# A two-layer hybrid decoder trunk: layer 1's first stage in a written order, the gate's mix made in the keys, the values' buffers opened at the layer's beginning

## The chip, the cores and the metric

The kernel runs on one core of a Trainium2 chip. Its engines each work through a queue of their own, in order: TensorE (PE) multiplies matrices, with the loads of its stationary operand shown apart as PEld; VectorE (DVE), ScalarE (ACT) and GpSimd (POOL) work on elements; SyncE (SP) issues nearly all the DMA transfers. The metric is the device time of one execution in microseconds (us). Three runs took 2486.44 to 2488.04 us, median 2487.72.

## What is computed

A sequence of 512 tokens of width 2048 (batch 1) passes through two layers. Layer 0 is an attention with forget gates. Layer 1 is RWKV-7 time mixing, cut here to what matters:

```
xx = shift(h) - h                       # the token before, minus this one
xr, xw, xk, xv, xa, xg = (h + xx * mu[i] for i in 0..5)
r, k, v, z = xr @ w_in[0], xk @ w_in[1], xv @ w_in[2], xg @ w_in[3]
decay = exp(-exp(-softplus(-(w0 + tanh(xw @ w1) @ w2)) - 0.5))
v = v + (v_first - v) * sigmoid(v0 + (xv @ v1) @ v2)     # v_first: layer 0's values
a = sigmoid(a0 + (xa @ a1) @ a2)
kk = normalised(k * k_k);  k = k * (1 + (a - 1) * k_a)
S = S * w_t + (S a_t) b_t + v_t k_t;  y_t = S r_t        # 512 steps, 32 heads of 64
y = groupnorm(y) + (r * k * r_k) summed * v
out = (y * silu(z)) @ w_out;  x = x + gate * out
```

`h` is the normalised `x`, scaled and shifted per channel by a modulation made from `c` (`w_mod`). All is float32.

## The kernel before, in words

Activations lie with channels on the 128 partitions: 16 tiles `k` of 128 channels by 512 tokens. Every large matmul is made of three in a faster format: operand and weight are each split into a high part (a copy by ACT, `hi` or `whi`) and a low part (the difference, by DVE, `lo` or `wlo`), and PE multiplies hi by hi, hi by wlo and lo by whi (`mm3`). Weights come by SP into `raw` buffers ahead of that. One output tile of a projection (128 channels) is 16 `mm3`, 48 matmuls, accumulated in one PSUM bank.

**Layer 1's first stage** (pool `st1`) goes over the 16 tiles `k`. Each step makes the normalised `xn` (DVE) and `hp` (ACT: `xn` plus shift, with a leading zero column, so that `hp[:, 0:T]` is the tokens one earlier), stores `hp` to the DRAM tensor `h1d`, makes the difference `d` (DVE) and from it three mixes: the key's, `d * mu + hp` on DVE, split into `A[k]`; and the receptance's (n = 0) and the gate's (n = 5), a product on ACT and an addition on POOL, stored to `mxd[1]` and `mxd[2]`. Then 18 matmuls use `A[k]` for the first six tiles of the key projection, in six PSUM banks at once (named `pj`, `x`, `S`). Its weights are the tensor `wst1`, 128 x 768 a step.

**Order.** For each engine the class `InOrder` can fix the order of the instructions as the program writes them (`e.on`). It is off in this stage, so that the scheduler orders it, and on before and after it.

**The rest of layer 1** is one stream of projection tiles for PE, written by `backbone`: 10 key tiles, 16 of the receptance (`wr`), 16 of the values (`wv1`), 16 of the gate (`wz1`), 16 of the output (`wo1`). Beside it run tasks (Python generators) that the planner `Flow` starts when its clock `fl.t` has reached their time. The clock counts PE's matmuls, and steps on by 0.2 where PE has none. A task's `yield 5` leaves 5 of these units before its next instructions. `backbone` gives a bank to tile `i` only when tile `i-2` is in `freed`. The task `side` goes through the phases, each with a pool of buffers of its own: the low-rank projections (`lora_k`; it also makes the values' mix), their second halves (`lora_up`), the keys (`keys`, started `KEY` = 9.8 units apart), and the recurrence (`stage`, `stage_half`, `chain`, pool `rk`), which opens when all `qd` are there.

- `keys(j)` loads the inner sums `ip`, the key `kt` and `aa`, makes normalised and decayed keys, stores them, and multiplies them into `gab`. After four keys, `invert` inverts small triangular blocks by elementwise work on POOL (on DVE for the last group, `DG`), tile `lane`, stored to `qld`. `inverse` then loads these into `qt` (SP) and finishes them with matmuls. It is started `INV` units after the group's last key, or `DINV + 8` for the last group.
- `values(j)` blends the values with layer 0's, in tiles `sv`, `vf` and `vt`, and stores `vvd` and `vtd`. Its buffers come from the pool `rk`, so it first waits for `vqs`, and it counts as ended for `freed` when its last instruction is written.
- `stage` loads what a head pair's recurrence needs (some 20 DMAs), among it `vtd`, for which it waits (`vd`). `chain(j)` is the recurrence of tile `j`: 8 chunks of 64 tokens, three hops each, a hop not before the next multiple of `HOP` = 2.15. A chain may start 12 hops after the one before. Its first operation reading PSUM is the copy `xs`, its end the copy `ys`, a norm, and the store to `ypd`.
- `gated(j)` multiplies `silu(z)` with `yp`; the output tiles need all 16 of these.
- `mixing(i, ...)` loads a stored mix back (`mxd`, tile `hp`, five buffers counted by the token `m`) and splits it for the projection; `premixed` says which are stored.

Of the kernel before, what the change touches and what calls it, by code (L numbers as in the profile page):

```python
# [17 lines left out]
P = 128  # L18
# [111 lines left out]
def body(ctx, tc, a, out, dbg=None, stop=0):  # L130
# [52 lines left out]
    mraw = cp.tile([P, 6, 2 * KT], F, name="mraw")  # L183
# [11 lines left out]
    pool.tensor_scalar(oka, vecs[:, V_KA, :], -1.0, 1.0, op0=OP.mult, op1=OP.add)  # L195
    lnb = cp.tile([P, 1], F, name="lnb")
# [67 lines left out]
    def mod_unit(mp, cb, l, part, t):  # L264
        for h in range(2):
            s = slice(h * D // 2, (h + 1) * D // 2)
            w = mp.tile([P, D // 2], F, tag="wm", name="wm", bufs=3)
            sp.dma_start(w, a["wmodT"][l, part * KT + t][:, s])
            yield 4.5
            dve.tensor_tensor_reduce(out=w, in0=w, in1=cb[:, s], scale=1.0, scalar=0.0,  # L270
                                     op0=OP.mult, op1=OP.add,
                                     accum_out=mraw[:, 3 * l + part, 2 * t + h:2 * t + h + 1])
            mdone.add((l, part, t, h))
        m0, m1 = (mraw[:, 3 * l + part, 2 * t + h:2 * t + h + 1] for h in range(2))
# [112 lines left out]
    with ExitStack() as s0:  # L387
# [209 lines left out]
        def until(i):  # L597
            while i is not None and i not in ends:
                yield 0.2
# [316 lines left out]
        for e in (pe, dve, act):  # L916
            e.on = False
# [13 lines left out]
        with tc.tile_pool(name="st1", bufs=2, reuse_waits="tile") as q:  # L931
            for k in range(KT):
                xp = q.tile([P, T + 1], F, tag="xn", name="xn")
                xn = xp[:, 1:]
                pool.tensor_scalar(xp[:, 0:1], shift[:, 1, k:k + 1], -1.0, 1.0, op0=OP.mult,
                                   op1=OP.mult)
                dve.scalar_tensor_tensor(out=xn, in0=x1[k], scalar=scale[:, 1, k:k + 1],
                                         in1=rstd1, op0=OP.mult, op1=OP.mult)
                hp = q.tile([P, T + 1], F, tag="hp", name="hp")
                pool.memset(hp[:, 0:1], 0.0)  # L940
                act.activation(hp[:, 1:], xn, AF.Identity, bias=shift[:, 1, k:k + 1])
                sp.dma_start(h1d[k], hp)
                w = wload(a["wst1"][k:k + 1].rearrange("k p n -> p k n"), 1, NS1, "s", q)
                A.append(new_act(k))
                d = q.tile([P, T], F, tag="d", name="d")
                dve.tensor_tensor(out=d, in0=xp[:, 0:T], in1=xn, op=OP.subtract)
                m = q.tile([P, T], F, tag="m", name="m")
                dve.scalar_tensor_tensor(out=m, in0=d, scalar=vecs[:, V_MU + 2, k:k + 1],
                                         in1=hp[:, 1:], op0=OP.mult, op1=OP.add)
# [19 lines left out]
    mq = ctx.enter_context(tc.tile_pool(name="mq", bufs=2, reuse_waits="tile"))  # L969
    pools = ExitStack()  # L970
# [75 lines left out]
    premixed = {(i, k) for i in (1, 2) for k in range(KT)}  # L1046
# [115 lines left out]
    def values(j, o, e):  # L1162
        while not vqs:
            yield 0.2
        vq = vqs[0]
# [3 lines left out]
        vv = load(vq, vfT[j], "vf", bufs=2)  # L1169
        yield from until(e)  # L1170
# [5 lines left out]
        dve.tensor_tensor(out=vv, in0=vv, in1=o, op=OP.add)  # L1176
        yield 3
# [13 lines left out]


# [3 lines left out]
    def keys(q, j):  # L1196
# [3 lines left out]
        yield 5  # L1200
# [429 lines left out]
    INV, KEY = 50, 9.8  # L1630

    def side(q):
# [45 lines left out]
        vqs.append(rk)  # L1678
# [25 lines left out]
    vqs = []  # L1704
# [40 lines left out]
```

## Time and profile before

| | before |
|---|---|
| median of 3 runs | 2487.72 us |
| profiled execution | 2484.87 us, its span 2483.2 us |
| mean granted TensorE clock | 0.979 |
| PE busy | 2342.1 us, 94%, 13626 matmuls |
| PEld | 1812.4 us, 73% |
| DVE | 1658.1 us, 67%, 3114 instructions |
| ACT | 1242.7 us, 50%, 2281 instructions |
| POOL | 756.2 us, 30%, 1199 instructions |
| DMA | 476.06 MB, mean 192 GB/s |

How to read its rows: a row of a timeline is start, duration, engine, line, operation, output<-inputs, shape, count; in brackets stands how long the engine was idle before it and what released it. A row of a group gives count, then busy time and mean ns of one, then the idle time before them. A row of a window gives the busy time of each engine with its instruction count. All instructions are issued through one helper, so that every row has its line, L88. PE's ends are modelled, and neighbouring matmuls overlap: their distance from start to start is what counts. In layer 1 the first stage lies near 1104 to 1207 us of the span, the keys near 1370 to 1612, the recurrence from 1700 on.

### The profile page before, as it was taken

Reading aid. Unit: us, or ns where it says so; the run is one execution under the profiler, and the core shown is the slowest. Engines: PE = TensorE matmul, PEld = TensorE weight load, DVE = VectorE, ACT = ScalarE, POOL = GpSimd, SP = SyncE. Lnnn points to the kernel's source line nnn. Section 1 sums busy time; section 2 is a strip of 40 time slices with the busy share of each in tenths; the row PEclk is TensorE's granted clock in tenths of the full one; section 3 lists DMA queues with packets and bytes.
Section 4 is the critical chain, followed back from the end, with each engine's and each line's share of the span. In section 5 each row is a group of like instructions: output and inputs, shape, how many; then the busy total and the mean of one; then the engine's idle time right before and its main releaser. Section 6 shows DMA issues by size and latency. Waiting matters only on the chain. (4 is left out here: it accounts for less than half of the span.)

```text
span 2483.2 us, 39895 instructions
## 1 busy us (share of the span) xinstructions
PE 2342.1 (94%) x13626; PEld 1812.4 (73%) x13626; DVE 1658.1 (67%) x3114; ACT 1242.7 (50%) x2281; POOL 756.2 (30%) x1199
## 2 busy tenths in 40 slices
PE   7998999999999999987999998887999999999999
PEld 4786677787777888865766776765777767777787
DVE  7878787888887553349796666572577876776332
ACT  3426655555556552226447676642344545555321
POOL 0003424433332200117340248720434444441000
PEclk8999999999999999999999999998999999999999
DMA  8856566666664275436657886776656656554453
GB/s 315 314 210 208 179 198 215 208 211 202 211 202 153 94 234 173 146 117 215 193 168 254 264 253 213 215 209 188 199 156 174 194 155 180 158 146 154 142 148 98
DMA packets 339260, 476.06 MB, mean 192 GB/s; under 512 B 146288, under 2 KB 156656, under 8 KB 335216
## 3 DMA queue, kind: packets, MB, share of 16 engines
q1 hardware_dynamic: 337392, 470.88, 60.5%
q0 software_dynamic: 1664, 2.63, 0.3%
q8 instruction: 108, 1.77, 0.3%
q14 instruction: 96, 0.79, 0.1%
HBM read 377.42 MB, written 95.95 MB: 191 GB/s over the span
## 5 line engine op out<-in xcount | busy, mean ns | idle before, releaser
L88 PE MATMUL pj<-hi,whi 128*128 128x512 f32 x2416 | 990.4, 410 | 16.8 <-ACT hi L88 10.3
L88 PE MATMUL pj<-hi,wlo 128*128 128x512 f32 x2416 | 954.7, 395 | 17.8 <-DVE wlo L88 17.8
L88 PE MATMUL pj<-lo,whi 128*128 128x512 f32 x2416 | 956.4, 396 | 2.3 <-DVE lo L88 2.3
L88 DVE TENSOR_TENSOR wlo<-raw,whi 128x512 fp32r<-128x512 f32 (+2 forms) x628 | 477.8, 768 | 278.5 <-ACT whi L88 276.0
L88 ACT ACTIVATE whi<-raw 128x512 fp32r<-128x512 f32 (+2 forms) x628 | 393.6, 634 | 412.6 <-PE pj L88 232.7
L88 PEld LDWEIGHTS pj<-hi,whi 128*128 128x128 f32 x2416 | 458.5, 190 | 122.7 <-ACT hi L88 11.6
L88 PEld LDWEIGHTS pj<-hi,wlo 128*128 128x128 f32 x2416 | 459.1, 190 | 108.3 <-DVE wlo L88 22.9
L88 PEld LDWEIGHTS pj<-lo,whi 128*128 128x128 f32 x2416 | 457.2, 189 | 104.1 <-DVE lo L88 3.4
L88 POOL TENSOR_SCALAR SV<-SV,dec 64x64 f32<-64x64 f32 x224 | 91.8, 410 | 221.7 <-DVE SV L88 207.3
L88 DVE CUSTOM_DVE_ANT_0 wm<-wm,cb 128x1024 f32<-128x1024 f32 x128 | 157.8, 1233 | 0.3
L88 ACT ACTIVATE pr<-Sm,mx 128x128 f32<-128x128 f32 (+3 forms) x128 | 71.5, 559 | 87.9 <-POOL mx L88 87.7
L88 POOL TENSOR_SCALAR mx<-mx 128x1 f32<-128x1 f32 x128 | 64.9, 507 | 158.2 <-DVE mx L88 110.0
L88 POOL TENSOR_SCALAR pr<-pr,rc 128x128 f32<-128x128 f32 (+3 forms) x128 | 96.0, 750 | 28.2 <-DVE rc L88 20.2
L88 DVE COPY SV<-x 64x64 f32<-64x64 f32 x256 | 56.6, 221 | 63.3 <-PE x L88 56.2
L88 DVE CUSTOM_DVE_ANT_0 Sm<-S,cmask 128x128 f32<-128x128 f32 (+3 forms) x128 | 62.1, 485 | 35.5 <-PE S L88 34.8
L88 POOL TENSOR_TENSOR lt<-lane 128x30 f32<-128x30 f32 (+14 forms) x90 | 61.3, 682 | 64.6 <-DMA lane<-mld 57.8
L88 DVE TENSOR_TENSOR SV<-SV,x 64x64 f32<-64x64 f32 x224 | 48.9, 218 | 37.9 <-PE x L88 32.3
L88 POOL TENSOR_TENSOR acc<-acc,sq 128x512 f32<-128x512 f32 x14 | 18.1, 1296 | 161.4 <-ACT sq L88 126.1
L88 POOL TENSOR_TENSOR lane<-lane,lt 128x30 f32<-128x30 f32 (+14 forms) x90 | 63.9, 710 | 7.1
L88 PE MATMUL S<-k,q 128*128 128x128 f32 (+7 forms) x256 | 62.7, 326 | 0.0
L88 PE MATMUL tr<-ident,pr 128*128 128x128 f32 x320 | 56.8, 275 | 4.6 <-ACT pT L88 1.6
L88 POOL TENSOR_TENSOR bk<-bk,eI 128x512 f32<-128x512 f32 x32 | 36.8, 1148 | 78.6 <-PE S L88 43.7
(321 smaller groups left out, 3439.6 us busy)
## 6 DMA issues: line engine op xcount, KB each, us to landing
wm<-in_wmodT SPq DMA_DIRECT2D x132, 512.0 KB, 4.3
raw<-in_wz SPq DMA_DIRECT2D x128, 256.0 KB, 3.8
raw<-in_wo SPq DMA_DIRECT2D x128, 256.0 KB, 3.5
raw<-in_wv SPq DMA_DIRECT2D x124, 256.0 KB, 3.7
wm<-in_wmodT SPq DMA_DIRECT2D x30, 1024.0 KB, 6.8
raw<-in_wk SPq DMA_DIRECT2D x96, 256.0 KB, 3.8
raw<-in_wr SPq DMA_DIRECT2D x64, 256.0 KB, 4.3
raw<-in_wq SPq DMA_DIRECT2D x56, 256.0 KB, 3.6
```

Source lines behind the costliest of these rows:

```text
L88: self.last = f(*a, **k)
```

## The change

- The engines stay in order through the first stage. Its loop is written out as small functions. Weights and `hp` are made up to two steps ahead; buffers are 3 for the weights' three tiles, 5 for `hp`.
- The mixes use `omu` = 1 - mu: `hp[before] * mu + hp * (1 - mu)`, the second product on ACT, the rest in one operation on DVE. `d` and POOL's additions go. The receptance's mix is made a step later (`mixr`), the gate's not at all here.
- `mixz(k)` makes the gate's mix in the keys' phase: a load of `h1d`, one operation on ACT, one on DVE, the store to `mxd[2]`. It is started 5 units after each key. The recurrence's pool opens when these are there too.
- The values' tiles come from a pool `vq` that is open from layer 1's beginning; `values` waits for its `svd` (`ups`) only, waits 5 units after its loads, and frees its bank after the last read.
- `keys` waits 8 units, not 5, after its loads; `INV` is 54, not 50; `mraw` has 4 rows of scratch, not 6.

```diff
-    mraw = cp.tile([P, 6, 2 * KT], F, name="mraw")
+    mraw = cp.tile([P, 4, 2 * KT], F, name="mraw")
...
+    omu = cp.tile([P, 3, KT], F, name="omu")
+    for i, n in enumerate((2, 0, 5)):
+        pool.tensor_scalar(omu[:, i, :], vecs[:, V_MU + n, :], -1.0, 1.0, op0=OP.mult,
+                           op1=OP.add)
...
-        for e in (pe, dve, act):
-            e.on = False
...
-            for k in range(KT):
-                xp = q.tile([P, T + 1], F, tag="xn", name="xn")
-                xn = xp[:, 1:]
-                pool.tensor_scalar(xp[:, 0:1], shift[:, 1, k:k + 1], -1.0, 1.0, ...)
+            def hidden(k):
+                xn = q.tile([P, T], F, tag="xn", name="xn")
                 dve.scalar_tensor_tensor(out=xn, in0=x1[k], scalar=scale[:, 1, k:k + 1],
                                          in1=rstd1, op0=OP.mult, op1=OP.mult)
-                hp = q.tile([P, T + 1], F, tag="hp", name="hp")
+                hp = hps[k] = q.tile([P, T + 1], F, tag="hp", name="hp", bufs=5)
                 pool.memset(hp[:, 0:1], 0.0)
                 act.activation(hp[:, 1:], xn, AF.Identity, bias=shift[:, 1, k:k + 1])
                 sp.dma_start(h1d[k], hp)
-                w = wload(a["wst1"][k:k + 1].rearrange("k p n -> p k n"), 1, NS1, "s", q)
+                g = gms[k] = q.tile([P, T], F, tag="g", name="g", bufs=3)
+                act.activation(g, hp[:, 1:], AF.Copy, scale=omu[:, 0, k:k + 1])
+            def mix(k):
+                m = mks[k] = q.tile([P, T], F, tag="m", name="m")
+                dve.scalar_tensor_tensor(out=m, in0=hps[k][:, 0:T],
+                                         scalar=vecs[:, V_MU + 2, k:k + 1], in1=gms.pop(k),
+                                         op0=OP.mult, op1=OP.add)
                 A.append(new_act(k))
-                d = q.tile([P, T], F, tag="d", name="d")
-                dve.tensor_tensor(out=d, in0=xp[:, 0:T], in1=xn, op=OP.subtract)
-                m = q.tile([P, T], F, tag="m", name="m")
-                dve.scalar_tensor_tensor(out=m, in0=d, scalar=vecs[:, V_MU + 2, k:k + 1], ...)
-                split(A[k][0], A[k][1], m)
-                for i, n in ((1, 0), (2, 5)):
-                    m = q.tile([P, T], F, tag=f"m{n}", name="m")
-                    act.activation(m, d, AF.Copy, scale=vecs[:, V_MU + n, k:k + 1])
-                    pool.tensor_tensor(out=m, in0=m, in1=hp[:, 1:], op=OP.add)
-                    sp.dma_start(mxd[i, k], m)
+                act_hi(A[k][0], m)
+            def mixr(k):
+                m = q.tile([P, T], F, tag="mr", name="mr")
+                hp = hps.pop(k)
+                act.activation(m, hp[:, 1:], AF.Copy, scale=omu[:, 1, k:k + 1])
+                dve.scalar_tensor_tensor(out=m, in0=hp[:, 0:T], scalar=vecs[:, V_MU, k:k + 1],
+                                         in1=m, op0=OP.mult, op1=OP.add)
+                sp.dma_start(mxd[1, k], m)
...
+            for k in range(3):
+                w_load(k)
+            w_hi(0); w_lo(0); hidden(0); mix(0); hidden(1); low(0); w_hi(1); w_lo(1)
+            for k in range(KT):
+                mix(k + 1)
+                hidden(k + 2)
+                low(k + 1)
+                w_load(k + 3)
+                w_hi(k + 2)
+                w_lo(k + 2)
+                mixr(k - 1)
+                w = ws.pop(k)
                 for i, o in enumerate(ks):
                     mm3(o, w, 0, A[k], k == 0, k == KT - 1, i * P, (i + 1) * P)
+            mixr(KT - 1)
...
+    vq = vst.enter_context(tc.tile_pool(name="vq", bufs=2, reuse_waits="tile"))
...
-    premixed = {(i, k) for i in (1, 2) for k in range(KT)}
+    premixed = {(1, k) for k in range(KT)}
...
     def values(j, o, e):
-        while not vqs:
+        while (j, 2) not in ups:
             yield 0.2
-        vq = vqs[0]
...
         vv = load(vq, vfT[j], "vf", bufs=2)
+        yield 5
         yield from until(e)
...
         dve.tensor_tensor(out=vv, in0=vv, in1=o, op=OP.add)
+        freed.add(e)
...
+    def mixz(q, k):
+        yield from take("m")
+        hp = load(mq, h1d[k], "hp", (P, T + 1), bufs=NHP)
+        yield 5
+        m = q.tile([P, T], F, tag="mm", name="m", bufs=2)
+        act.activation(m, hp[:, 1:], AF.Copy, scale=omu[:, 2, k:k + 1])
+        yield 1.5
+        dve.scalar_tensor_tensor(out=m, in0=hp[:, 0:T], scalar=vecs[:, V_MU + 5, k:k + 1],
+                                 in1=m, op0=OP.mult, op1=OP.add)
+        free["m"] += 1
+        yield 1.5
+        sp.dma_start(mxd[2, k], m)
+        premixed.add((2, k))
...
         aa = load(q, aad[j], "aa", bufs=2)
-        yield 5
+        yield 8
...
-    INV, KEY = 50, 9.8
+    INV, KEY = 54, 9.8
...
             fl.start(fl.t, keys(kp, j))
+            fl.start(fl.t + 5, mixz(kp, j))
             yield KEY
-        while len(qd) < KT:
+        while len(qd) < KT or len(premixed) < 3 * KT:
             yield 0.2
```

`low(k)` is the split's subtraction of the key's mix; `w_load`, `w_hi` and `w_lo` are the load of `wst1` and its split.

More of the change, by code (lines that the diff above doesn't have):

```diff
@@ L271, in mod_unit @@
                                      op0=OP.mult, op1=OP.add,
-                                     accum_out=mraw[:, 3 * l + part, 2 * t + h:2 * t + h + 1])
+                                     accum_out=mraw[:, 3 * l + part - 2, 2 * t + h:2 * t + h + 1])
             mdone.add((l, part, t, h))
-        m0, m1 = (mraw[:, 3 * l + part, 2 * t + h:2 * t + h + 1] for h in range(2))
+        m0, m1 = (mraw[:, 3 * l + part - 2, 2 * t + h:2 * t + h + 1] for h in range(2))
         b = vecs[:, V_BM + 3 * l + part, t:t + 1]
@@ L931, in body, with w_load, w_hi @@
         with tc.tile_pool(name="st1", bufs=2, reuse_waits="tile") as q:
-            for k in range(KT):
-                xp = q.tile([P, T + 1], F, tag="xn", name="xn")
-                xn = xp[:, 1:]
-                pool.tensor_scalar(xp[:, 0:1], shift[:, 1, k:k + 1], -1.0, 1.0, op0=OP.mult,
-                                   op1=OP.mult)
+            rws, ws, xns, hps, gms, mks = ({} for _ in range(6))
+            def w_load(k):
+                if k < KT:
+                    rws[k] = q.tile([P, 1, NS1], F, tag="raws", name="raw", bufs=3)
+                    sp.dma_start(rws[k], a["wst1"][k:k + 1].rearrange("k p n -> p k n"))
+            def w_hi(k):
+                if k < KT:
+                    hi = q.tile([P, 1, NS1], R, tag="whis", name="whi", bufs=3)
+                    act_hi(hi, rws[k])
+                    ws[k] = hi, q.tile([P, 1, NS1], R, tag="wlos", name="wlo", bufs=3)
+            def hidden(k):
+                if k >= KT:
+                    return
+                xn = q.tile([P, T], F, tag="xn", name="xn")
                 dve.scalar_tensor_tensor(out=xn, in0=x1[k], scalar=scale[:, 1, k:k + 1],
                                          in1=rstd1, op0=OP.mult, op1=OP.mult)
-                hp = q.tile([P, T + 1], F, tag="hp", name="hp")
+                hp = hps[k] = q.tile([P, T + 1], F, tag="hp", name="hp", bufs=5)
                 pool.memset(hp[:, 0:1], 0.0)
@@ L942, in body @@
                 sp.dma_start(h1d[k], hp)
-                w = wload(a["wst1"][k:k + 1].rearrange("k p n -> p k n"), 1, NS1, "s", q)
-                A.append(new_act(k))
-                d = q.tile([P, T], F, tag="d", name="d")
-                dve.tensor_tensor(out=d, in0=xp[:, 0:T], in1=xn, op=OP.subtract)
-                m = q.tile([P, T], F, tag="m", name="m")
-                dve.scalar_tensor_tensor(out=m, in0=d, scalar=vecs[:, V_MU + 2, k:k + 1],
-                                         in1=hp[:, 1:], op0=OP.mult, op1=OP.add)
@@ new lines, in mix @@
+            def mix(k):
+                if k >= KT:
+                    return
+                m = mks[k] = q.tile([P, T], F, tag="m", name="m")
+                dve.scalar_tensor_tensor(out=m, in0=hps[k][:, 0:T],
+                                         scalar=vecs[:, V_MU + 2, k:k + 1], in1=gms.pop(k),
+                                         op0=OP.mult, op1=OP.add)
+                A.append(new_act(k))
+                act_hi(A[k][0], m)
+            def mixr(k):
+                if k < 0:
+                    return
+                m = q.tile([P, T], F, tag="mr", name="mr")
[4 more added lines that the diff above has]
+                sp.dma_start(mxd[1, k], m)
@@ new lines, in w_lo, with low @@
+            def w_lo(k):
+                if k < KT:
+                    dve.tensor_tensor(out=ws[k][1], in0=rws.pop(k), in1=ws[k][0],
+                                      op=OP.subtract)
+            def low(k):
+                if k < KT:
+                    dve.tensor_tensor(out=A[k][1], in0=mks.pop(k), in1=A[k][0],
+                                      op=OP.subtract)
+            for k in range(3):
+                w_load(k)
+            w_hi(0)
+            w_lo(0)
+            hidden(0)
@@ L956, in body @@
+            mix(0)
+            hidden(1)
+            low(0)
+            w_hi(1)
+            w_lo(1)
+            for k in range(KT):
[7 more added lines that the diff above has]
+                w = ws.pop(k)
                 for i, o in enumerate(ks):
                     mm3(o, w, 0, A[k], k == 0, k == KT - 1, i * P, (i + 1) * P)
+            mixr(KT - 1)
@@ L969, in body @@
     mq = ctx.enter_context(tc.tile_pool(name="mq", bufs=2, reuse_waits="tile"))
+    vst = ExitStack()
+    ctx.callback(vst.close)
+    vq = vst.enter_context(tc.tile_pool(name="vq", bufs=2, reuse_waits="tile"))
     pools = ExitStack()
@@ L1677, in side @@
         rk = pools.enter_context(tc.tile_pool(name="rk", bufs=1, reuse_waits="tile"))
-        vqs.append(rk)
         for i in range(4):
@@ L1702, in side @@
             yield 0.1
-    vqs = []
     fl.start(0, side(q))
```

## The prediction

> **What bounds the kernel now.** I read the stretches of the span first, to find where TensorE (PE) is not busy, then for each such place the groups by shape, each engine's timeline and the waits.
>
> ```profile
> 1100.00:1200.00 100.00, 74.10 (x277) 54.57 (x276) 85.08 (x85) 55.21 (x85) 61.32 (x62) 0.90 0.61 196
> ...
> 1370.00:1612.00 242.00, 216.04 (x1461) 168.24 (x1460) 152.89 (x197) 168.45 (x312) 140.79 (x193) 0.95 0.77 234
> ...
> 1700.00:1800.00 100.00, 83.48 (x526) 63.04 (x528) 46.49 (x100) 29.31 (x54) 32.18 (x72) 0.90 0.70 197
> ```
>
> After the length the columns are PE, weight loads, DVE, ACT and POOL busy, granted clock, DMA share, GB/s. PE bounds the kernel nearly everywhere (94% of the span busy, by the table above). The change works on three stretches where it idles: layer 1's first stage (26 us of PE idle in 1100 to 1200), the keys (26 idle of 242), and the start of the recurrence (16.5 idle in 1700 to 1800).
>
> ```profile
> 1114.05 0.79 PE L88 MATMUL pj<-hi,whi 128*128 128x512 f32 x1 [8.18 <-ACT hi L88]
> ...
> 1195.05 0.39 PE L88 MATMUL pj<-hi,whi 128*128 128x512 f32 x1
> ...
> 1206.71 0.40 PE L88 MATMUL S<-lo,whi 128*128 128x512 f32 x1
> ...
> L88 POOL TENSOR_TENSOR m<-m,hp 128x512 f32<-128x512 f32 x32 | 50.4, 1592 | 3.6 <-ACT m L88 3.4
> ...
> L88 DVE TENSOR_TENSOR lo<-m,hi 128x512 fp32r<-128x512 f32 x16 | 20.5, 1296 | 0.0
> ...
> L88 DVE SCALAR_TENSOR_TENSOR xn<-x,scale,rs 128x512 f32<-128x512 f32 x16 | 19.0, 1214 | 0.0
> ...
> L88 DVE SCALAR_TENSOR_TENSOR m<-d,vecs,hp 128x512 f32<-128x512 f32 x16 | 16.4, 1043 | 0.1
> ...
> L88 DVE TENSOR_TENSOR wlo<-raw,whi 128x768 fp32r<-128x768 f32 x13 | 14.9, 1149 | 0.4 <-ACT whi L88 0.4
> ...
> L88 DVE TENSOR_TENSOR d<-xn 128x512 f32<-128x512 f32 x16 | 12.3, 792 | 0.0
> ...
> PE pj L88 <- DVE wlo L88: 14.7, 9, 3.1
> ```
>
> The stage runs from 1114.05 to 1206.94 (the last row and 0.23): 92.9 us, 5.8 for each of its 16 steps. In its end, where nothing is late, 50 matmuls lie between 1195.05 and 1206.71: 0.233 us each, so 18 of a step need 4.2 us and all 288 need 67.2. DVE is never idle: 1.296 + 1.214 + 1.043 + 1.149 + 0.792 = 5.5 us a step. DVE sets the pace and PE waits for its `wlo`.
>
> **First stage.** POOL's two additions a step go (the gate's to the keys, the receptance's to DVE); DVE loses `d` and gains `mixr`'s operation, so it has five as before. ACT has five as before (`hp`, `g`, `whi`, `hi`, `mixr`'s product). The SP queue loses one store a step. What DVE and ACT need one by one, where POOL is not in their way:
>
> ```profile
> 1136.86 0.68 DVE L88 TENSOR_TENSOR lo<-m,hi 128x512 fp32r<-128x512 f32 x1
> ...
> 1138.06 0.74 DVE L88 SCALAR_TENSOR_TENSOR xn<-x,scale,rs 128x512 f32<-128x512 f32 x1
> 1138.73 0.74 DVE L88 SCALAR_TENSOR_TENSOR m<-d,vecs,hp 128x512 f32<-128x512 f32 x1
> 1139.39 1.58 DVE L88 TENSOR_TENSOR d<-xn 128x512 f32<-128x512 f32 x1
> ...
> 1139.54 0.62 ACT L88 ACTIVATE hi<-m 128x512 fp32r<-128x512 f32 x1
> 1140.06 0.71 ACT L88 ACTIVATE m<-d,vecs 128x512 f32<-128x512 f32 x1
> 1140.67 0.71 ACT L88 ACTIVATE hp<-xn,shift 128x512 f32<-128x512 f32 x1
> ...
> 1199.39 0.84 ACT L88 ACTIVATE whi<-raw 128x768 fp32r<-128x768 f32 x1 [4.64 <-DMA raw<-in_wst]
> ...
> 1200.27 0.96 DVE L88 TENSOR_TENSOR wlo<-raw,whi 128x768 fp32r<-128x768 f32 x1 [4.52 <-ACT whi L88]
> ```
>
> Independent neighbours on one engine start 0.6 to 0.67 us apart, and from ACT's end to DVE's start lie 0.04 us. DVE's sum falls to 0.67 x 3 + 0.6 + 0.87 = 3.5 us a step, below PE's 4.2. But the order is now fixed, and it holds a loop: on DVE `mix`, `xn`, `low`, `wlo`, `mixr`, where `wlo` waits for a `whi` that stands on ACT behind `hp` and `g`, and these wait for `xn`. From `mix` at 0: `xn` 0.67 to 1.41; `hp` 1.45 to 2.16; `g`, which reads it, 2.20 to 2.91; `whi` 2.81 to 3.65; `wlo` from 3.69; `mixr` 0.87 later, 4.56; the next `mix` 0.66 later. A step takes 5.2 us, and DVE's wait for `whi` is what is late next.
>
> The start: `wlo` of step 0 now stands between the norm and `xn`, 0.87 us more; from the norm's end at 1109.43 (row below), `wlo` 0.87, `xn` 0.75, `hp` 0.71, `g` 0.71, `mix` 0.74, `hi` 0.63 and five handovers of 0.04 give the first matmul at 1114.0, as before. `xn`, `hp`, `g`, `whi`, `wlo` of step 1 follow, so `mix` of step 1 starts near 1117.1 and that of step 2, with no `mixr` between, 4.55 later. Thirteen steps of 5.2 later `mix` of step 15 starts at 1189.3, its `hi` ends at 1190.7, and 18 matmuls end at 1194.9: **12 us earlier**. The ends: at PE's own pace 67.2 us and 3.4 for the half-clock matmuls of the start (8 at 0.43 instead of 0.23, and their waits), hence 22 saved; with 0.15 more at each of the loop's four handovers the step is 5.8 and nothing is saved; a loss of 4 if it is 6.1. I take the loop, because each of its members has a row.
>
> ```profile
> 1108.74 0.69 DVE L88 SCALAR_TENSOR_TENSOR rs<-rs1u,rs 128x512 f32<-128x512 f32 x1
> ...
> POOL on L88 <- DVE scale L88: 134.7, 1, 134.7
> ```
>
> The three `omu` operations stand on POOL at the kernel's start, ahead of the second row's wait of 134.7 us: nothing; uncovered they would cost three short operations, under 2 us. The smaller `mraw` costs nothing.
>
> **The keys.** Each key gets `mixz`: one ACT operation (0.71), one on DVE (0.74), a load of `h1d` and the store taken from the first stage. ACT is busy 168 of 242 us, DVE 153, so 11.4 and 11.8 us more fit into their idle time: the lower end is 0. All of it on the path is 23 us. I take 4, 0.25 a key: PE idles 11% of this stretch, and only then does an operation ahead in ACT's queue count in full. The added issues on SP, two of 0.32 to 0.5 us a key, have weights queued behind them; their waits are the third rival.
>
> `INV` goes from 50 to 54. It sets when the loads of an inverted group enter SP's queue:
>
> ```profile
> 1512.14 3.77 SPq L88 DMA_DIRECT2D qt<-qld  x8
> 1516.01 0.39 SPq L88 DMA_DIRECT2D raw<-in_wr  x1
> ...
> 1509.12 0.63 POOL L88 DMA_DIRECT2D qld<-lane  x1 [0.30 <-POOL lane L88]
> ...
> 1519.50 0.63 ACT L88 ACTIVATE whi<-raw 128x512 fp32r<-128x512 f32 x1 [5.87 <-DMA raw<-in_wr]
> ...
> 1526.76 0.79 PE L88 MATMUL S<-mhi,blkr 128*128 128x512 f32 x1 [6.84 <-ACT mhi L88]
> ...
> SPq L88 <- DMA qld<-lane: 17.6, 3, 8.6
> ...
> L88 SPq DMA_DIRECT2D ypd<-dc x16: 319/326/437, 1828.7 to 2313.6; - x16
> ```
>
> SP stands up to 8.6 us before `qt<-qld`, because POOL issues the first `qld` at 1509.12 only; the weights behind it come late, ACT waits 5.87 us and PE 6.84. Four units of the planner are about 5 us here: chains, 25.8 units apart (12 hops of 2.15), end 32.3 us apart by the last row, (2313.6 - 1828.7)/15. So 5 of the 8.6 go: I take **4 us saved**, between 0 (POOL's inversion gets as much longer) and 8 (the second group's stall too). The longer `yield` in `keys` moves the last key, and with it the recurrence, by 3 units, 3.7 us.
>
> The Trainium skill's page "SBUF — State Buffer", section "Who interferes with whom", speaks against this part: a DVE instruction with two SBUF inputs and a GpSimd instruction that reads SBUF hold each other up in full. `mixz`'s DVE operation is of this kind, and POOL's inversions run beside it. The trace agrees with the page (the 0.68 and 1.58 us above, for one shape); by it the 12 `mixz` beside POOL's inversions cost up to 0.9 us more each, 11 in all, and were these all on the path the time would be 2477.
>
> **Values.** They no longer wait until the keys' buffers close:
>
> ```profile
> 1708.98 1.11 PE L88 MATMUL S<-ident,vf 128*128 128x128 f32 x4 [11.31 <-DVE vf L88]
> 1711.88 0.90 PE L88 MATMUL S<-ident,vf 128*128 128x128 f32 x3 [1.78 <-DVE vf L88]
> ...
> 1754.16 0.23 DVE L88 COPY xs<-x 128x64 f32<-128x64 f32 x1
> ...
> 2302.51 0.60 ACT L88 ACTIVATE ys<-y 128x512 f32<-128x512 f32 x1 [0.69 <-PE y L88]
> ...
> 2320.85 158.50 PE pj L88 x690
> ```
>
> PE's two waits are 13.1 us; with the next value tiles running they go. The chain of waits ends in 158.5 us of output tiles, which start when the last chain is through. Chains keep their 32.3 us whatever PE has beside them, so what counts is when the first chain starts (1754.16). It comes 13.1 us earlier by the stalls and 2 by matmuls that need not run at half clock after them, and later by the 3.7 us of the longer keys; 1 I leave for the clock at the end, where PE now runs out of tiles: the 56 matmuls moved ahead (13.1/0.233) are missing between 2302.51 and 2320.85, beside the last chain's norm. **10 us saved.** The ends: 0, if SP's staging loads set the first chain as they do now, and 17, if the longer keys are hidden too.
>
> **The sum**: 12 + 10 + 4 - 4 = 22 us. The profiled execution took 2484.87 us, 1.7 more than its span; the median of the runs is 2.9 above it, and the saving is taken from the median: 2487.7 - 22 = 2466.
>
> **The rivals**, after the rows that the third and the fifth use (SP's waits; stretches of 5 us with the granted clock as the third column from the end):
>
> ```profile
> SPq L88 <- DVE bk L88: 25.9, 12, 4.8
> ...
> 1114.00:1119.00 5.00, 2.69 (x6) 1.68 (x7) 5.00 (x4) 1.96 (x4) 4.94 (x6) 0.50 0.43 161
> ...
> 1139.00:1144.00 5.00, 3.64 (x16) 2.66 (x15) 5.00 (x5) 3.61 (x6) 4.56 (x5) 1.00 0.64 222
> ...
> 1169.00:1174.00 5.00, 5.00 (x16) 3.92 (x15) 5.00 (x6) 2.42 (x4) 3.60 (x5) 0.66 0.74 236
> ```
>
> 1. PE sets the first stage: `hi`, `hp` and `whi` overlap better than I chained them. For it: DVE's and ACT's sums are below 4.2. Then 22 there and 14 at the values, 4 at `INV`, 4 lost: 2452.
> 2. The values' part gives nothing, since the first chain waits for SP's staging loads either way and PE loses its tiles at the end. For it: PE's output tiles start only 18 us after the last chain's `ys`; against: 13 us in which PE does nothing. 2476.
> 3. Slower: the gate's mix blocks SP in the keys. Its store waits for DVE at the head of SP's queue, as the key's own store does (25.9 us in 12 waits, 2.2 each). Sixteen of 2.2 are 35 us with the weights behind: 2487.7 - 26 + 35 = 2497. It decides above 1.6 us a key. Against: three weight tiles are loaded ahead.
> 4. The order does nothing: the loop takes 5.8, and the values' gain is returned at the end: 2484 to 2488.
> 5. Slower by the clock: PE idles 1 us in every step, and the clock falls to half. At half clock a matmul takes 0.43, a step 7.7 and the stage 123 us: 30 more instead of 12 less, 2508. Against: at 1139 to 1144, with 1.36 us idle, the clock stayed at 1.00; at 1169, behind the longest wait of 3.1 us, it was 0.66. The Trainium skill's page "TensorE: Matmul & The Clock Gate", section "HAM oscillation — how this bites in real kernels", has a kernel that is throttled at every tile by gaps of more than about 3.4 us; by that rule gaps of 1 us are safe, and the trace agrees, though its clock fell somewhat earlier, at 3.1.
>
> **How the numbers follow.** My forecast 0.46 (its own range 2458 to 2475), first rival 0.20, second 0.18, third 0.08, fourth 0.06, fifth 0.02. The range reaches from the first rival with some of its bounds, 2447, to the second with a dearer gate mix, 2482. Within 0.2% (5 us, about what a measurement of this kernel can tell) lie the fourth and a little of the second: 0.08; slower 0.09; faster 0.83.
>
> **What would show it.** First stage: POOL nearly empty, DVE's `lo` at 0.68, PE waiting about 1 us a step for `hi` or `lo`, the last S matmul near 1195 on this scale; at 1185 the first rival holds. Keys: SP's wait before the first `qt<-qld` near 4 us. Values: no wait of PE on `vf`, the first `xs` copy 20 to 25 us earlier in the span, a gap of PE between the last `ys` and the output tiles. I am wrong if the keys' stretch grows by over 10 us or the first `xs` moves less than 15.

## The result and the profile after

The changed kernel takes 2502.24 us (median of 4 runs, 2499.37 to 2505.41) against 2487.88 for the kernel before; the ratio is 1.0059, with an interval of 1.0041 to 1.0076. It is slower by 14.7 us, where 22 us of gain were forecast. Its profiled execution has a span of 2503.5 us against 2483.2, 20.3 more.

Below, a difference in us between two versions is the difference of their ratios to the kernel before, times 2487.7. A ratio compares a run with executions of the kernel before from the same session, which a median does not, so the two can differ by 2 us or so.

The stretches of the changed kernel at the times that the prediction showed for the kernel before (length, then PE, weight loads, DVE, ACT and POOL busy, granted clock, DMA share, GB/s):

```profile
1100.00:1200.00 100.00, 85.01 (x328) 60.45 (x327) 60.30 (x82) 56.02 (x82) 3.42 (x13) 0.95 0.44 142
1370.00:1612.00 242.00, 223.72 (x1429) 172.04 (x1428) 173.78 (x214) 183.21 (x334) 136.86 (x185) 0.99 0.88 278
1700.00:1800.00 100.00, 88.58 (x554) 67.99 (x553) 40.65 (x77) 31.33 (x61) 22.76 (x55) 0.88 0.71 199
```

In all three PE is busier than before (85.0 against 74.1, 223.7 against 216.0, 88.6 against 83.5), as was meant, and yet the kernel ends later. Four points of the trace say where. First, layer 0, which the change does not touch. A stretch of 100 us in which PE has nothing but projection tiles, before and then after:

```profile
1000.00:1100.00 100.00, 100.00 (x438) 82.07 (x437) 36.45 (x44) 25.82 (x44) 11.67 (x9) 1.00 0.43 140
```

```profile
1000.00:1100.00 100.00, 100.00 (x432) 81.07 (x431) 37.04 (x45) 26.46 (x45) 11.68 (x9) 1.00 0.42 142
```

The clock is 1.00 in both, PE never waits, and 432 matmuls go through instead of 438: 0.2315 us each instead of 0.2283. Second, the first stage and what stands behind it (PE's timeline, with the idle time in brackets):

```profile
1124.08 0.79 PE L88 MATMUL pj<-hi,whi 128*128 128x512 f32 x1 [8.19 <-ACT hi L88]
...
1143.68 0.50 PE L88 MATMUL pj<-hi,whi 128*128 128x512 f32 x1 [0.51 <-ACT hi L88]
...
1148.91 0.50 PE L88 MATMUL pj<-hi,whi 128*128 128x512 f32 x1 [0.52 <-ACT hi L88]
...
1206.83 0.40 PE L88 MATMUL S<-lo,whi 128*128 128x512 f32 x1
1216.65 0.80 PE L88 MATMUL pj<-hi,whi 128*128 128x512 f32 x1 [9.43 <-ACT kt L88]
```

The stage starts 10.0 us later than before (1114.05), takes 83.0 us instead of 92.9, and is followed by a wait of 9.43 us that the kernel before does not have. Third, the first `xs` and the chains, fourth the output tiles:

```profile
L88 DVE COPY xs<-x x128: 214/225/226, 1779.8 to 2319.4; 128x64 f32<-128x64 f32 x128
```

```profile
L88 SPq DMA_DIRECT2D ypd<-dc x16: 319/326/480, 1853.0 to 2330.0; - x16
```

```profile
2336.24 163.44 PE pj L88 x690
```

The sum of the 20.3 us: 10.0 in layer 0; -0.3 from the stage's first matmul to the next tile's (1216.65 - 1124.08 = 92.6, before 92.9 without a gap); 15.9 from there to the first `xs` (563.1 instead of 547.2); -5.3 from the first `xs` to the end (723.7 instead of 729.0). In that last part the chains lie 31.8 us apart, (2330.0 - 1853.0)/15, instead of 32.3, which gives 8 back, and the 690 matmuls of the output tiles take 163.44 instead of 158.50, which takes 5. Their first rows, before and then after:

```profile
2320.85 0.50 PE L88 MATMUL pj<-hi,whi 128*128 128x512 f32 x1 [2.17 <-ACT hi L88]
```

```profile
2336.24 0.80 PE L88 MATMUL pj<-hi,whi 128*128 128x512 f32 x1 [9.24 <-ACT hi L88]
2336.84 0.63 PE L88 MATMUL pj<-hi,wlo 128*128 128x512 f32 x1
2337.26 0.63 PE L88 MATMUL pj<-lo,whi 128*128 128x512 f32 x1
```

Behind the longer wait the first 15 start 0.43 us apart, which is half clock, and by estimate costs 3 us; the rest is 690 times the 0.0032 us of layer 0.

### The profile page after: what moved, and what is told of

Same layout as the page of the kernel before. It is cut to its first block, busy times and chain, and to the rows that moved or that the text cites. A ratio compares the mean times of both kernels' runs of the same rounds, so it can differ in the third digit from the quotient of the medians.

```text
span 2503.5 us, 39838 instructions
## 1 busy us (share of the span) xinstructions
PE 2364.5 (94%) x13626; PEld 1812.8 (72%) x13626; DVE 1649.2 (66%) x3130; ACT 1257.2 (50%) x2299; POOL 700.3 (28%) x1154
## 4 chain that ended last, share of the span: by engine, by line
PE 70%; DVE 10%; POOL 6%; ACT 5%; DMA 4%; issue 4%; SPq 1%; DVEq 0%; ACTq 0%; POOLq 0%
PE pj L88 55%; PE S L88 6%; PE x L88 3%; POOL lane L88 3%; POOL lt L88 3%; PE tr L88 2%; DVE m L88 2%; DVE wlo L88 2%; PE pv L88 2%; PE y L88 1%; SPq L88 1%; PE ss L88 1%; ACT whi L88 1%; DVE wm L88 1%; DMA raw<-in_wv 1%
## 5 line engine op out<-in xcount | busy, mean ns | idle before, releaser
L88 POOL TENSOR_TENSOR lt<-lane 128x30 f32<-128x30 f32 (+14 forms) x90 | 63.4, 705 | 56.1 <-DMA lane<-mld 49.3
L88 PE MATMUL S<-k,q 128*128 128x128 f32 (+7 forms) x256 | 62.3, 324 | 0.0
```

The costliest lines, as they stand in the source:

```text
L88: self.last = f(*a, **k)
```

## The experiments: layer 0 and the addresses

The built programs give the reason for layer 0 a name. In each partition the weights' buffers `whi` begin at byte 28832 before and at 28768 in the changed kernel: `mraw` is 256 bytes shorter, `omu` takes 192, and every pool on that side moves 64 down. The activations `hi` and `lo` lie in pools on the other side and stay (first `hi` at 163808). Call the first minus the second, modulo 256, the distance: 192 before, 128 after. The first run makes this part of the change alone, on the kernel before.

```diff
-    mraw = cp.tile([P, 6, 2 * KT], F, name="mraw")
+    mraw = cp.tile([P, 4, 2 * KT], F, name="mraw")
...
+    omu = cp.tile([P, 3, KT], F, name="omu")      # and its three operations; nothing reads it
```

> The kernel before with one small part of the change alone: mraw with 4 rows and the tile omu with its three operations, which nothing reads. Every pool that lies behind the constants, the weights' buffers among them, starts 64 bytes lower in each partition; nothing else differs. Theory A (TensorE's pace depends on where the weights lie): pure stretches of projection tiles show 432 matmuls in 100 us instead of 438, layer 1's first matmul comes 10 us later (1124 instead of 1114), and the whole is 10 to 20 us slower than before, 2498 to 2508. Theory B (the later start of layer 1 is something else, the first stage's order or chance): within 3 us of before, 2485 to 2491, first matmul of layer 1 near 1114.

2500.21 us, ratio 1.0047 (1.0034 to 1.0060): 11.7 of the 14.7 us, from a tile that is made smaller and one that nobody reads. The same 100 us of it:

```profile
1000.00:1100.00 100.00, 100.00 (x432) 81.04 (x432) 36.22 (x45) 26.45 (x45) 11.66 (x9) 1.00 0.43 142
```

Then the reverse, on the changed kernel:

```diff
+    cp.tile([P, 16], F, name="pad")               # 64 bytes; in the next run 8 for 16
```

> The changed kernel with 64 bytes of padding behind omu, so that the weights' buffers lie where they lay before; nothing else differs from it. Theory A: layer 1's first matmul back to 1114, and 10 to 15 us less than the changed kernel, 2487 to 2492: the rest of the change then gains nothing. Theory B: no change, 2502.

2486.64 us, ratio 0.9995 (0.9981 to 1.0010). Theory A holds: 15.9 us go with 64 bytes that hold nothing (the intervals of this figure and of the 11.7 overlap), and the rest of the change is worth 1, which the interval does not tell from nothing.

```profile
1000.00:1100.00 100.00, 100.00 (x439) 82.04 (x438) 37.58 (x46) 26.46 (x45) 11.64 (x9) 1.00 0.43 143
```

> The same with 32 bytes of padding: the weights' buffers then begin at a multiple of 128 bytes (before 32 beyond one, in the changed kernel 96 beyond one, as the activations do). If what costs is the same offset as the activations', this is as quick as 64 bytes of padding, 2487 to 2492; if the distance from a multiple of 128 counts, it is quicker still, by up to 10; theory B: 2502.

2502.51 us, ratio 1.0059 (1.0045 to 1.0074), so nothing is gained, and both guesses on the offset were wrong: a start at a multiple of 128 bytes is no better. (The time is that of theory B, which the run before had ruled out.)

```profile
1000.00:1100.00 100.00, 100.00 (x430) 80.44 (x429) 36.72 (x45) 26.45 (x45) 11.67 (x9) 1.00 0.43 141
```

Is it the weights' own place or the distance? In the next run the weights stay where the change put them, and the activations move.

```diff
     def act_pool(name, bufs):
         ast.close()
+        ast.enter_context(tc.tile_pool(name="rp", bufs=1, side="right")).tile([P, 16], F, ...)
```

> The changed kernel without padding on the side of the weights, but with 64 bytes in the pools on the other side, where the activations (hi, lo) lie: these begin 32 beyond a multiple of 128 bytes, the weights 96 beyond one, the reverse of before. If the distance of the two counts (64 apart is quick, 0 and 32 apart slow): 438 matmuls in 100 us, layer 1's first matmul 10 us earlier than in the changed kernel, 2485 to 2490. If the weights' own offset counts: 432, 2500 to 2504.

2485.82 us, ratio 0.9999 (0.9990 to 1.0008), 438 matmuls in the 100 us: it is the distance. Three later runs, on the best version of the next section (ratio 0.9895, distance 192), gave its rule; `omu` was moved to other pools and the constants were cut or padded.

> The best version so far (2460.65 us) with omu in other pools and the constants smaller, so that the weights' buffers begin 0 bytes beyond the activations' counted modulo 512 (before 192, changed kernel 128). What the runs show so far: 192 gives 438 matmuls in 100 us, 128 gives 432, 160 gives 430; in the first stage, whose weights have offsets of their own, 256 gave 0.227 us a matmul, 192 gave 0.229, 320 gave 0.233. If the pattern repeats every 256 bytes: 0 is as quick as 256, 441 or more in 100 us, layer 1's first matmul some 6 us earlier, 2448 to 2455. If it repeats every 512 or more, 0 is not known: slow like 128 it would cost 15, 2475.

2451.98 us, ratio 0.9856 (0.9841 to 0.9871), 9.7 us less than the version with 192.

```profile
1000.00:1100.00 100.00, 100.00 (x443) 82.84 (x442) 36.10 (x44) 25.83 (x44) 11.63 (x9) 1.00 0.42 142
```

> The same without any padding: distance 448 modulo 512, 192 modulo 256. If the pattern repeats every 256 bytes: 438 matmuls in 100 us as with 192, 2459 to 2463. If not: another pace, 430 to 434 and 2470 to 2478 for a slow one.

2460.09 us, ratio 0.9892 (0.9871 to 0.9912), 438 matmuls: as with 192, so the pattern repeats after 256.

> The best version so far with the constants 96 bytes smaller than with the padding: distance 96. Between 128 (432) and the 64 modulo 256 of the first stage before (0.233): 429 to 432 matmuls in 100 us, 2472 to 2478. If the slow band ends at 128, 434 to 438 and 2460 to 2468.

2471.92 us, ratio 0.9952 (0.9930 to 0.9973), 428 matmuls, just below the first expectation's. Last, distance 0 on the kernel before, with nothing else of the change but the smaller `mraw`:

> The kernel before with one thing changed: mraw with 4 rows and 64 bytes of padding, so that the weights' buffers begin 0 bytes beyond the activations' modulo 256 (before 192). If the distance is a matter of TensorE's pace alone, and nothing of the change is needed for it: 443 matmuls in 100 us, and 6 to 12 us less than before, 2476 to 2482. If the gain of 8.7 us that the distance 0 gave in the best version rests on that version's shorter stalls: under 4 us.

2480.64 us, ratio 0.9973 (0.9963 to 0.9984): 6.7 us less than before, again with 443 matmuls.

| distance (bytes, modulo 256) | matmuls in 1000 to 1100 us | us each |
|---|---|---|
| 0 | 443, 443 | 0.2257 |
| 192 | 438, in one version 439 | 0.2283 |
| 160 | 430 | 0.2326 |
| 128 | 432, 432 | 0.2315 |
| 96 | 428 | 0.2336 |

The first stage's own weights bear this out. Their distance was 64 in the kernel before, where the prediction read 0.233 us a matmul off the trace and took that for PE's pace; in the run with the smaller `mraw` on the kernel before it is 0, and one step reads

```profile
1210.80 0.39 PE L88 MATMUL x<-hi,whi 128*128 128x512 f32 x1
...
1213.29 0.39 PE L88 MATMUL S<-lo,whi 128*128 128x512 f32 x1
```

whose starts lie eleven matmuls apart, 0.226 each.

Layer 0's first stage bears it out a third time, and its traces hold the two distances that are missing. Its weight tiles are 672 columns wide, so that the built programs have two distances there, 128 apart. Taken from the starts of neighbours without a wait, its mean is 0.2275 us at 0 and 0.2337 at 128 in the last run; 0.2333 at 32 in the run with 32 bytes of padding; and 0.2322 at 224 in the run with distance 96 (mostly six matmuls in a row, such as those that start from 108.56 to 109.72 us and from 126.83 to 127.99). So 0 is the quickest, 192 the next, and the other six lie at 0.231 to 0.234. Why, no run shows.

## The experiments: the rest of the change

All of these have the 64 bytes of padding, so that the distance is 192 as before.

**The wait behind the first stage.** What stands ahead of `kt` on ACT in the changed kernel, and SP's queue at the same time:

```profile
1204.20 0.72 ACT L88 ACTIVATE mr<-hp,omu 128x512 f32<-128x512 f32 x1 [1.56 <-DMA mxd<-mr]
1208.65 0.72 ACT L88 ACTIVATE mr<-hp,omu 128x512 f32<-128x512 f32 x1 [3.73 <-DMA mxd<-mr]
1209.28 1.65 ACT L88 ACTIVATE whi<-raw 128x512 fp32r<-128x512 f32 x3
1215.49 0.63 ACT L88 ACTIVATE whi<-raw 128x512 fp32r<-128x512 f32 x1 [4.55 <-DMA raw<-in_wk]
1216.02 1.07 ACT L88 ACTIVATE kt<-pj 128x512 f32<-128x512 f32 x2
```

```profile
1203.88 6.63 SPq L88 DMA_DIRECT2D mxd<-mr  x3
1210.79 1.53 SPq L88 DMA_DIRECT2D raw<-in_wk  x3
```

The receptance's mix has two buffers; the last two products wait until stores have landed, and behind them wait, on ACT, the weights' copies and `kt`, and on SP the next weights.

```diff
-                m = q.tile([P, T], F, tag="mr", name="mr")
+                m = q.tile([P, T], F, tag="mr", name="mr", bufs=4)
```

> 64 bytes of padding, and four buffers instead of two for the receptance's mix in the first stage. In the changed kernel TensorE waits 9.4 us behind this stage for the copy kt, which stands on ScalarE behind the last two products of that mix, and these wait for the stores of earlier ones to land. Theory: that wait goes, with the 2 us at half clock behind it, and 8 to 11 us are saved against the same padding alone, 2477 to 2483. Rival: the copies kt wait for weights or for the queue of stores anyway, and less than 4 us are saved.

2481.59 us, ratio 0.9971 (0.9961 to 0.9980): 6.0 us less than with the padding alone, between theory and rival. The stores no longer hold ACT, but the fourth weight's load is still late, and PE still waits 6.1 us for `kt`:

```profile
1192.76 1.93 ACT L88 ACTIVATE mr<-hp,omu 128x512 f32<-128x512 f32 x3
1194.59 1.66 ACT L88 ACTIVATE whi<-raw 128x512 fp32r<-128x512 f32 x3
1203.20 0.63 ACT L88 ACTIVATE whi<-raw 128x512 fp32r<-128x512 f32 x1 [6.95 <-DMA raw<-in_wk]
```

This version (0.9971) is the base of the next runs.

**The loop of the first stage**, with `whi` and the receptance's product ahead of `hp` and `g` on ACT:

```diff
                 mix(k + 1)
+                w_hi(k + 2)
+                mixr_a(k - 1)          # the product on ACT, taken out of mixr
                 hidden(k + 2)
                 low(k + 1)
                 w_load(k + 3)
-                w_hi(k + 2)
                 w_lo(k + 2)
                 mixr(k - 1)
```

> The changed kernel with 64 bytes of padding and four buffers for the receptance's mix (2481.6 us, the base of this row of runs), and in the first stage's loop the weight's copy whi and the receptance's product stand on ScalarE ahead of hp and g, not behind them. Theory (a step is paced by the loop mix, xn, hp, g, whi, wlo, mix): the loop falls below TensorE's 4.2 us, a step takes 4.2 to 4.4 instead of 5.23, and the last matmul of the stage comes 11 to 13 us earlier; the time falls by 8 to 13 us, 2469 to 2474. Rival (what comes behind the stage waits for weights and stores that the queues bring no earlier): the stage ends earlier, the wait for kt grows by as much, and less than 4 us are saved.

2471.03 us, ratio 0.9929 (0.9912 to 0.9946): 10.4 us less. PE's timeline has no wait left in a step, and a step takes 4.12 us, PE's own 18 x 0.229:

```profile
1141.37 0.39 PE L88 MATMUL pj<-hi,whi 128*128 128x512 f32 x1
...
1145.49 0.39 PE L88 MATMUL pj<-hi,whi 128*128 128x512 f32 x1
...
1192.36 0.80 PE L88 MATMUL pj<-hi,whi 128*128 128x512 f32 x1 [4.56 <-ACT kt L88]
```

**The values.** First their old timing whole, then only its wait:

```diff
-        while (j, 2) not in ups:
+        while not vqs:                 # until the recurrence's pool is open
             yield 0.2
...
-        yield 5                        # this line and the next in the first run only
...
-        freed.add(e)
```

> The base (2481.6 us) with the values' timing as before: they wait until the recurrence's buffers are open, without the 5 units behind their loads, and their bank counts as free when their last instruction is written; their buffers stay where they are. Prediction's theory: TensorE's wait of about 13 us for vf is back and the first xs comes 8 to 10 us later, 2490 to 2492. Rival (the staging's loads set the first chain either way): the first xs stands within 4 us, the chains are again 32.3 us apart instead of 31.7, and the time is 2 to 9 us longer through that, 2484 to 2490. Second rival: nothing is lost, 2480 to 2483.

> The base (padding, four mr buffers; 2481.6 us) with one part of the values' old timing alone: they wait again until the recurrence's buffers are open; the 5 units behind their loads and the early free bank stay as in the change. Theory C (value tiles that start early put a tile of 48 matmuls and four more weight loads between the last qtd and the first x of the recurrence): this part alone gives what all the old timing gave, 2470 to 2474, first xs 10 us earlier than in the base. Theory D (the bank that is free earlier, or the 5 units, does it): 2479 to 2484.

2471.57 us, ratio 0.9941 (0.9921 to 0.9960), and 2471.16, ratio 0.9940 (0.9927 to 0.9954). No expectation of the first of the two held, the prediction's least: the old timing is *better* by 7.5 us. PE waits 2.6 us for `vf` there, not 13, and the first `xs` comes 10.6 us earlier than in the base. The wait alone does it (7.7), as theory C had it. The time between the last `qtd` and the first `xs`, with the projection's matmuls that PE does in it: the kernel before, the changed kernel, the base, and the run with the old wait.

```profile
1699.30:1754.20 54.90, 29.50 (x109) 0.81 0.73 204
```

```profile
1714.70:1779.80 65.10, 45.66 (x158) 0.82 0.73 199
```

```profile
1700.10:1758.80 58.70, 41.21 (x156) 0.88 0.79 216
```

```profile
1692.70:1742.30 49.60, 35.45 (x132) 0.90 0.77 211
```

The kernel before does 109 matmuls there, the changed one 158, a whole tile of 48 more. These need weights, whose loads stand in SP's queue between the staging's. ACT's waits in the same two stretches, before and after:

```profile
ACT whi L88 <- DMA raw<-in_wv: 19.4, 4, 5.9
```

```profile
ACT whi L88 <- DMA raw<-in_wv: 38.7, 9, 7.6
```

The matmuls that are done early are missing later. PE's idle time behind the first stage (from 1207 us; in the changed kernel from 1216.65), up to the first `xs` and from there to the output tiles:

| | up to the first `xs` | from there to the output tiles |
|---|---|---|
| before | 62.3 us | 12.9 |
| changed | 48.3 | 24.3 |
| base | 49.6 | 24.2 |
| base, old timing | 54.2 | 12.5 |
| base, old wait alone | 46.9 | 16.5 |

The gap ahead of the recurrence is filled, and a gap of nearly that size opens at its end, where the last chain runs alone: between the start of its `ys` and the output tiles PE is busy for 3.0 of 15.2 us in the base, and for 15.5 of 18.8 with the old timing.

**INV**, back to 50 on the base:

> The base (2481.6 us) with INV back at 50. Prediction's theory: SyncE's wait before the first load of an inverted group grows from 3 to 7 or 8 us, weights come late, and the time is 2 to 6 us longer, 2484 to 2488. Rival (the wait is covered by weights loaded ahead, and the recurrence starts earlier by 4 units of the planner): the same or up to 4 us shorter, 2478 to 2482.

2491.93 us, ratio 1.0018 (1.0006 to 1.0031): 11.7 us more, about twice what the prediction's theory allowed. The path is the one that the prediction read: SP stands before `qt<-qld`, the weights behind it come late, and with them, on ACT, the split of a key's squares, for which PE waits. SP's own wait is not much longer, 5.0 us at most instead of 3.1; what differs is its place. With 50 it stands ahead of a weight load that is issued before it with 54 (SP's queue with 50, then in the base):

```profile
1515.52 3.77 SPq L88 DMA_DIRECT2D qt<-qld  x8
...
1520.81 0.95 SPq L88 DMA_DIRECT2D raw<-in_wr  x1
```

```profile
1516.13 1.51 SPq L88 DMA_DIRECT2D raw<-in_wr  x1
...
1521.44 3.78 SPq L88 DMA_DIRECT2D qt<-qld  x8
```

What follows in the run with 50, on ACT and on PE:

```profile
1525.91 0.63 ACT L88 ACTIVATE whi<-raw 128x512 fp32r<-128x512 f32 x1 [8.42 <-DMA raw<-in_wr]
```

```profile
1528.95 0.80 PE L88 MATMUL S<-mhi,blkr 128*128 128x512 f32 x1 [5.99 <-ACT mhi L88]
```

It is not the only one. Of PE's waits from 1500 to 1712 us, those for the split squares, in the run with 50 and then in the base (total, times, longest):

```profile
PE S L88 <- ACT mhi L88: 8.4, 4, 6.0
...
PE S L88 <- DVE mlo L88: 5.9, 4, 3.3
```

```profile
PE S L88 <- DVE mlo L88: 4.2, 5, 1.6
...
PE S L88 <- ACT mhi L88: 0.3, 1, 0.3
```

These two are 14.3 us against 4.5, all of PE's waits there 21.3 against 15.5. The run with 50 has three stretches of 20 us in which the mean granted clock is 0.74, the base none below 0.89. The clock seems to be the greater part: from 1207 us to the output tiles PE idles 74.8 us with 50 and 73.9 in the base, and the mean clock up to the last `qtd` is 0.96 against 0.99. The two profiled executions lie 5.8 us apart, though, not 11.7, so the whole of the price is not accounted for.

**The gate's mix:**

```diff
-            fl.start(fl.t + 5, mixz(kp, j))
...
+    premixed = {(i, k) for i in (1, 2) for k in range(KT)}     # and mxd[2, k] read from h1d
```

> The base (2481.6 us) without any mix of the gate: its loads, products and stores in the keys are left out, and the gate's projection reads the unmixed h, so that its values are not the reference's. Prediction's theory: the mixes cost 4 us there, 2477 to 2478. Rivals: they are hidden, 2481 to 2482; they block SyncE's queue, and over 10 us come back, below 2472.

2477.09 us, ratio 0.9955 (0.9941 to 0.9968): the sixteen mixes cost 4.0 us, a difference near the limit of what the intervals tell.

**Together.** Padding, the values' old timing and INV 50 (two mr buffers, the written order):

> The changed kernel with 64 bytes of padding, the values' old timing and INV at 50: what stays of the change is the ordered first stage with its two buffers for mr, the gate's mix in the keys, the longer yield in keys, and the values' buffers in a pool of their own. If the parts add (values +10, INV -10.3, as measured on the base): 2486.6 - 10.0 + 10.3 = 2487, no change against before. If INV earns its 10 us only where value tiles run ahead: 2475 to 2480. Prediction's sum for these parts: 2487.7 - 12 + 4 = 2480, less up to 10 for the wait for vf.

2488.99 us, ratio 1.0006 (0.9996 to 1.0015), 1.5 us over before: the parts add. Then the gains together:

> What the runs so far point to: padding, four mr buffers, whi ahead of hp in the first stage's loop, the values' old timing; INV 54 and the gate's mix in the keys as in the change. If the gains add: 2471.0 - 10.0 = 2461, 26 below before. If the values' gain shrinks where the keys end earlier: 2465 to 2471.

2460.65 us, ratio 0.9895 (0.9882 to 0.9908), where the ratios of its parts add to 0.9899. With distance 0, above, it is 2451.98: 36 us below the kernel before and 50 below the changed one.

## Why the prediction was wrong

| part | predicted | measured | from |
|---|---|---|---|
| smaller `mraw`, `omu` | 0 | +15.9 | changed kernel against 64 bytes of padding |
| values | -10 | +7.5 | old timing on the base |
| first stage | -12 | -1.0 | what remains; -7.0 with four mr buffers |
| INV 54 | -4 | -11.7 | INV 50 on the base |
| gate's mix in the keys | +4 | +4.0 | left out on the base |
| sum | -22 | +14.7 | |

The first stage's figure is the remainder: it holds whatever else is left (the longer `yield` in `keys`, predicted within the values' part, was not tried alone) and the errors of all the others. The run with only it, the gate's mix and the buffers tests it: 1.5 measured, 3.0 by the table.

**"The smaller `mraw` costs nothing"** is the step that failed most, and it made the kernel slower; without it the change would have been worth 1 us. I priced the tile by its instructions, and did not ask what moves when a tile at the bottom of a stack shrinks. The price is PE's pace, 1.4% of every projection matmul outside the first stages. The page before lists 7248 of them (`pj`), which by this estimate would be 23 us; not all of it reaches the end of the kernel.

**Values: right on the stall, wrong on what it was worth.** The wait for `vf` did go (11.31 us before, 2.0 at most after; with the old timing on the base 2.6), but the first `xs` came 25.6 us later in the span, not 20 to 25 earlier. The first failed step is "It comes 13.1 us earlier by the stalls and 2 by matmuls that need not run at half clock". I took PE's idle time for time on the path to the first chain. That path leads through the last `qtd`, the staging's loads on SP, and the weights that are queued between them. Where the planner has no matmul, its clock steps on for nothing; with value tiles allowed early, the same units of the staging are filled with matmuls, and PE, in order, has to do 48 more with four or five more late weights ahead of the first `x`. The second failed step is the "1 I leave for the clock at the end". There PE's wait is 9.24 us instead of 2.17 and half clock follows; from the first `xs` to the output tiles it idles 11.4 us more than before, against 14.0 less ahead of the first `xs`. The second rival named both, the loads and the tiles that are missing at the end, but thought the part indifferent, 2476; in fact it costs. What did help may be the pool of their own for the values' buffers: with it, the old timing and INV 50 (the first run under "Together") the stretch from the last `qtd` to the first `xs` is 49.3 us instead of 54.9. No run moves the pool alone. The trace also contradicts "Chains keep their 32.3 us whatever PE has beside them": with value tiles gone ahead they are 31.8 apart (31.7 in the base, 32.1 there with the old timing).

**First stage: the loop right, its end forgotten.** 5.23 us a step (5.2 predicted), DVE's wait for `whi` is what is late,

```profile
1145.91 0.96 DVE L88 TENSOR_TENSOR wlo<-raw,whi 128x768 fp32r<-128x768 f32 x1 [1.56 <-ACT whi L88]
1146.79 0.75 DVE L88 SCALAR_TENSOR_TENSOR mr<-hp,vecs,mr 128x512 f32<-128x512 f32 x1
1147.45 0.75 DVE L88 SCALAR_TENSOR_TENSOR m<-hp,vecs,g 128x512 f32<-128x512 f32 x1
```

POOL is nearly empty (3.4 us in 100), `lo` takes 0.69 in the loop, and the last S matmul, less the 10.0 us of layer 0, stands at 1196.8 (1195 predicted). PE's wait in a step is 0.5 us by the brackets, but by the starts, which are what counts, a step is 5.23 and its 18 matmuls at 0.233 take 4.2: 1 us, as forecast. The stage is 9.9 us shorter; the 12 of the sum stopped at its last matmul, and the next tile starts no earlier, since the mixes that trail behind the loop hold ACT and SP. The change thus added a wait, and the prediction had not named what is queued behind it. The first rival, a stage at PE's pace, was not what the change does; with two calls moved it is.

**INV: right mechanism, size too small.** SP's wait before the first `qt<-qld` fell as forecast:

```profile
SPq L88 <- DMA qld<-lane: 3.8, 1, 3.8
```

(17.6 in three waits before). The step that failed is "So 5 of the 8.6 go": it prices one wait of SP, and what hangs on it are several waits of PE, with the half clock behind them. **The gate's mix** cost its 4 us. The dearer case for it, 0.9 us more for each DVE operation beside POOL's inversions, did not come: the sixteen take 0.74 to 1.14 us each, 2.5 us more in all. The third rival's condition, more than 1.6 us a key, was not met, and the clock did not fall within the stage, so the fifth was not either. What came out is none of the five rivals: I had no case in which layer 0 changes.

The Trainium skill's page "SBUF — State Buffer", section "A bandwidth-pool intuition that's wrong (but worth ruling out)", gives TensorE a second, independent read port for weight loads. One could take from it that the place of the weights against the activations does not matter; of addresses it says nothing. These runs show that the place matters: 443 matmuls in 100 us at distance 0 and 428 at 96, at the same granted clock of 1.00.

## What to carry to other kernels

Before two versions of a TensorE-bound kernel are compared, compare the pace of their undisturbed matmul streams. Where it differs, compare the addresses: here a few bytes of padding put both on one footing. Try the handful of distances in steps of 32 bytes early; from 192 to 0 gave 9.7 us on the best version here, about what moving two calls in the first stage's loop gave (10.4).

An idle engine is not a stall to be filled until the chain to the next late thing is followed: work that is moved into the gap goes ahead of that chain in an in-order queue, with its loads, and is missing where it was taken from. And a stage ends where the next one starts: look at what trails behind the last matmul on each queue.

## What was not expected of the hardware

At full granted clock, with no wait, a stream of 128x512 matmuls on split fp32 operands (fp32r in the rows that make them) ran at 0.2257 to 0.2336 us each, by the distance of the stationary operand's buffer from the moving one's modulo 256 bytes: 3.5% between 0 and 96. 0 and 192 were quick, the other multiples of 32 slow. The pattern held in three parts of the kernel and under both ways of moving (weights or activations); 32, 64 and 224 were seen only in the layers' first stages (0.233, 0.233 and 0.232). What causes it stays open.
